# Three experts with few tokens: 64 slots and plain float32 products on two column tiles

## The chip, the core and the metric

The kernel runs on one core of a Trainium2 chip. The metric is the device time of one launch in microseconds, as the median of three runs. The engines are named as in the profile: PE (TensorE's products) and PEld (its weight loads), DVE (VectorE), ACT (ScalarE), POOL (GpSimd) and SP (SyncE, which issues the weight DMAs).

## What is computed

Two transformer blocks on 256 tokens of width 1024, in float32. The change lies in the mixture of experts of the first block's second layer:

```python
N_EXPERTS, TOP_K, D_EXPERT = 8, 2, 3584
def _moe(h, router, w1, w3, w2):
    logits = (hf @ router).astype(jnp.float32)
    top_v, top_i = lax.top_k(logits, TOP_K)
    top_w = jax.nn.softmax(top_v, axis=-1)
    gates = jnp.sum(jax.nn.one_hot(top_i, N_EXPERTS, dtype=jnp.float32) * top_w[..., None], axis=-2)
    for e in range(N_EXPERTS):
        y = y + gates[:, e:e + 1] * (jax.nn.silu(hf @ w1[e]) * (hf @ w3[e])) @ w2[e]
```

Each token goes to two of eight experts, so 512 token places are shared out unevenly. All of an expert's weights, 42 tiles of 1 MB, are read whatever its number of tokens.

## The kernel before

Weights come in tiles of 128 x 2048 float32 (1024 KB), each by one DMA that SP issues (`unit`, L238) into the next of `MOE_RING` = 6 buffers `raw`. SP works in order, so a load waits until the buffer's earlier contents are used up. Ordinary products use float32r: `split` makes of 1024 columns a rounded part `wh` (ACT, L245) and the rest `wl` (DVE, L246), four buffers of each, and `mm3` (L257 to L259) adds three products wh·xH, wl·xH, wh·xL. A `raw` buffer is free when its two halves are split.

`moe` ranks the experts: rank 0 is expert 0 whatever its count (`FIRST`), ranks 1 to 7 are the others by falling count. Rank 1 has 128 slots and 32 more (`CAP1` = 160), all others 128. `gather` (L1011) collects the tokens' rows in slots by products with a 0/1 matrix S and ACT evictions (L1024); `parts` (L1027) splits the rows in xeH and xeL (L1033, L1034); two ranks share a gather (`pair`, L1168).

`expert` (L1043) is a generator with one step per 512 hidden columns, seven in all and a rest. A step has four weight tiles for gate and up (48 products of 512 columns into two PSUM banks), SiLU (ACT, L1083), the multiplication (DVE, L1085), then two tiles of the down product for the step before (24 products), four transposes of the new hidden columns (L1109) and their split (L1112, L1113). The outputs are split and wait in `late`; `settle` multiplies them back to the tokens (L1148, L1149) while the next products run, and DVE adds them to y (L1158).

The 32 extra slots of rank 1 use another kind of product, plain float32 straight from `raw`: the stationary operand has 32 columns and the output takes 32 of PSUM's 128 partitions, so that four such products stand on four column tiles of the array (L1079 with 128 columns, L1103 with 256):

```python
for j in range(4):
    o = (kc % 4) * 512 + j * 128
    nc.tensor.matmul(px[32 * j:32 * j + 32, z * 128:(z + 1) * 128], xex[:, kc, :],
                     raw[:, o:o + 128], start=(kc == 0), stop=(kc == 7))
```

Order: rank 0 alone for five steps, then ranks 2 to 7 one after another, and after every fifth of their steps one step of rank 1 (L1201 to L1209). `ready` gathers an expert's rows before the last products of the one ahead of it (`run(g)`, L1203). After the stage the norms follow, and under `If(over > 0)` (L1245) a second pass of an expert whose tokens don't fit its slots, with a single weight buffer (`spare`).

Of the kernel before, what the change touches and what calls it, by code (L numbers as in the profile page):

```python
# [24 lines left out]
class Cols:  # L25
    """Columns of the small-parameter tile, in the order they are packed."""
# [30 lines left out]
def pack(inp):  # L57
# [42 lines left out]
    u = []  # L100
# [32 lines left out]
    for e in range(8):  # L133
# [15 lines left out]
        np.broadcast_to(np.where(r8 == 1, CAP1, 128).astype(np.float32), (128, 8))], axis=1)  # L149
# [65 lines left out]
CAP1 = 160  # L215
FF2_ORDER = [0, 2] + [u for i in range(2, 16) for u in (2 * i, 2 * i - 3)] + [29, 31]
# [4 lines left out]
class K:  # L221
# [19 lines left out]
    def split(self, src, n):  # L241
        """Exact split of fp32 data in two float32r parts."""
# [19 lines left out]
    def rsqrt(self, v, n):  # L262
        """1/sqrt(v) on [128, n] by Newton steps from the bit-pattern estimate."""
# [15 lines left out]
    def inv_rms(self, v, width):  # L279
        """1/sqrt(v / width) of a column v."""  # L280
# [18 lines left out]
    def diag(self, ys):  # L299
        """The diagonal matrices of two columns."""  # L300
# [18 lines left out]
def run(gen, n=None):  # L319
    """Advance a generator by n steps, or to its end."""  # L320
# [6 lines left out]
def ada_part(k, l, i):  # L327
    """Columns i*2048.. of silu(c) @ w_ada[l] + b_ada[l], for c (row 0) and c_ctx (row 1); a step per weight tile."""
# [31 lines left out]
def mod_cols(k, l, s):  # L360
    """A = g*(1+scale), B = shift as columns [128, 8, 2] for the s-th norm of layer l."""
# [8 lines left out]
class Sums:  # L370
    """Sums of squares of token rows, a column per half row."""
# [16 lines left out]
    def diag(self, t):  # L388
        """diag(1 / rms(x)) of token tile t."""
# [7 lines left out]
def mod_T(k, sums, A, B, H, L, by_tile=True):  # L397
    """Transposed A*xn + B of the four token tiles in two float32r parts; A, B: column 0 for x, 1 for ctx."""
# [288 lines left out]
def gain_T(k, ps, g, H, L):  # L687
    """Two float32r parts of ps * g (g per partition)."""
# [208 lines left out]
def moe(k):  # L897
# [12 lines left out]
    def order(v, lead, name):  # L910
        """How many entries come before each: greater ones, and equal ones of lower index."""
# [973 lines left out]
```

## Time and profile before

| | |
|---|---|
| median of three runs | 2372.45 us (2371.38 to 2373.67) |
| the profiled execution, its own span | 2374.5 us, 2.05 over the median |
| PE busy | 2290.1 us, 96% |
| PEld busy | 1810.7 us, 76% |
| DVE busy | 1736.9 us, 73% |
| ACT busy | 1282.0 us, 54% |
| DMA | 554.58 MB, mean 234 GB/s over the span |
| weight tiles of the experts | 336 of 1024.0 KB, 5.4 us from issue to landing |

The profile is of one execution. Busy shares are averages over stages with different limits, and PE's busy time overlaps itself, since a product's record is longer than the spacing between two of them. So the starts of neighbouring records tell TensorE's pace, and waits tell which engine or queue is ahead of which. A plain float32 product appears as two records.

### The profile page before, as it was taken

The page shows a single profiled execution, that of the slowest core. Times are in us where ns is not written, and L with a number is a line of the kernel's source. Part 1 is how long each engine was busy: PE and PEld are TensorE (multiplying, and loading weights), DVE is VectorE, ACT ScalarE, POOL GpSimd, SP SyncE. Part 2 cuts the span into 40 slices and gives each one's busy share as a digit, 9 for nine tenths or more (in the row PEclk, how much of TensorE's full clock was granted, in tenths as well). Part 3 has the DMA queues.
Part 4 walks back from the last instruction along what each step waited for, and adds up shares of the span by engine and source line. Part 5 has one row for each costly group of instructions (what it writes and reads, how often), then busy time and mean ns, then how long its engine had stood idle before and what let it go on. Part 6 is the DMA issues. An engine that isn't in the chain of part 4 may idle for free. (4 is left out here: it accounts for less than half of the span.)

```text
span 2374.5 us, 32425 instructions
## 1 busy us (share of the span) xinstructions
PE 2290.1 (96%) x12225; PEld 1810.7 (76%) x12225; DVE 1736.9 (73%) x2665; ACT 1282.0 (54%) x1709; POOL 49.5 (2%) x98
## 2 busy tenths in 40 slices
PE   6999999999999899999999999999999799999998
PEld 3767877788876777787877777778768587798997
DVE  3997359443665888897878788879788778776555
ACT  3234322222454677776767676767667644554444
POOL 1000000000000000000000000000000000000000
PEclk8999999999999999999999999999999899999999
DMA  9544445332540687897988888979779643344552
GB/s 371 225 162 162 180 151 195 129 124 91 201 169 32 235 340 299 300 374 280 366 316 323 309 343 327 359 283 353 306 267 362 254 158 111 125 146 156 190 188 78
DMA packets 82116, 554.58 MB, mean 234 GB/s; under 512 B 9904, under 2 KB 10160, under 8 KB 19232
## 3 DMA queue, kind: packets, MB, share of 16 engines
q1 hardware_dynamic: 75600, 531.87, 60.0%
q0 software_dynamic: 6208, 19.52, 2.4%
q8 instruction: 98, 1.61, 0.3%
q10 hardware_dynamic: 144, 1.05, 0.1%
q14 instruction: 66, 0.54, 0.1%
HBM read 546.08 MB, written 6.32 MB: 233 GB/s over the span
## 5 line engine op out<-in xcount | busy, mean ns | idle before, releaser
L246 DVE TENSOR_TENSOR wl<-raw,wh 128x1024 fp32r<-128x1024 f32 (+1 forms) x916 | 1097.5, 1218 | 371.1 <-ACT wh L245 360.7
L245 ACT CAST wh<-raw 128x1024 fp32r<-128x1024 f32 (+1 forms) x916 | 948.0, 1047 | 756.0 <-PE psA L259 217.7
L258 PE MATMUL psA<-wl,xeH 128*128 128x512 f32 x784 | 312.2, 398 | 2.1 <-DVE wl L246 2.1
L257 PE MATMUL psA<-wh,xeH 128*128 128x512 f32 x784 | 313.1, 400 | 0.4 <-ACT xf L1024 0.2
L259 PE MATMUL psA<-wh,xeL 128*128 128x512 f32 x784 | 310.5, 396 | 0.1
L258 PE MATMUL psO<-wl,hidH 128*128 128x512 f32 x480 | 190.7, 397 | 1.6 <-DVE wl L246 1.6
L259 PE MATMUL psO<-wh,hidL 128*128 128x512 f32 x480 | 189.8, 396 | 0.2 <-DVE hidL L1113 0.2
L257 PE MATMUL psO<-wh,hidH 128*128 128x512 f32 x480 | 185.1, 397 | 1.9 <-ACT hidH L1112 1.9
L258 PEld LDWEIGHTS psA<-wl,xeH 128*128 128x128 f32 x784 | 147.6, 188 | 40.9 <-DVE wl L246 7.4
L257 PEld LDWEIGHTS psA<-wh,xeH 128*128 128x128 f32 x784 | 147.7, 188 | 35.3 <-issue 0.6
L259 PEld LDWEIGHTS psA<-wh,xeL 128*128 128x128 f32 x784 | 147.6, 188 | 35.4 <-DVE xeL L1034 0.5
L257 PE MATMUL psG<-hH,wh 128*128 128x256 f32 x544 | 157.8, 290 | 0.9 <-DVE hL L690 0.9
L257 PE MATMUL psA<-xTH,wh 128*128 128x512 f32 x400 | 157.3, 393 | 0.0
L259 PE MATMUL psG<-hH,wl 128*128 128x256 f32 x544 | 155.8, 286 | 0.0
L258 PE MATMUL psA<-xTL,wh 128*128 128x512 f32 x400 | 155.7, 389 | 0.0
L259 PE MATMUL psA<-xTH,wl 128*128 128x512 f32 x400 | 155.7, 389 | 0.0
L258 PE MATMUL psG<-hL,wh 128*128 128x256 f32 x544 | 155.1, 285 | 0.0
L257 PEld LDWEIGHTS psG<-hH,wh 128*128 128x128 f32 x544 | 103.9, 191 | 13.2 <-issue 11.2
L257 PEld LDWEIGHTS psO<-wh,hidH 128*128 128x128 f32 x480 | 90.5, 189 | 24.9 <-ACT hidH L1112 2.3
L259 PEld LDWEIGHTS psG<-hH,wl 128*128 128x128 f32 x544 | 104.0, 191 | 6.3 <-issue 6.2
L258 PEld LDWEIGHTS psO<-wl,hidH 128*128 128x128 f32 x480 | 90.4, 188 | 22.7 <-DVE wl L246 2.0
L259 PEld LDWEIGHTS psO<-wh,hidL 128*128 128x128 f32 x480 | 90.5, 189 | 21.4 <-DVE hidL L1113 0.6
(564 smaller groups left out, 3664.8 us busy)
## 6 DMA issues: line engine op xcount, KB each, us to landing
raw<-in_moe_dram SPq DMA_DIRECT2D x336, 1024.0 KB, 5.4
raw<-in_w_ada_dram SPq DMA_DIRECT2D x48, 1024.0 KB, 6.1
raw<-in_w2ff_dram SPq DMA_DIRECT2D x32, 1024.0 KB, 4.8
raw<-in_w2mix_dram SPq DMA_DIRECT2D x24, 1024.0 KB, 4.9
raw<-in_eff_dram SPq DMA_DIRECT2D x22, 1024.0 KB, 4.9
raw<-in_eff_dram SPq DMA_DIRECT2D x22, 512.0 KB, 3.5
raw<-in_ein_dram SPq DMA_DIRECT2D x8, 1024.0 KB, 8.2
raw<-in_w2in_dram SPq DMA_DIRECT2D x8, 1024.0 KB, 4.9
```

The costliest lines, as they stand in the source:

```text
L245: self.nc.scalar.copy(h[:, :n], src)
L246: self.nc.vector.tensor_sub(l[:, :n], src, h[:, :n].bitcast(F32))
L257: mm(ps, s[0], m[0], start=first, stop=False)
L258: mm(ps, s[0], m[1], start=False, stop=False)
L259: mm(ps, s[1], m[0], start=False, stop=last)
```

## The change

Ranks 5, 6 and 7 (`SMALL`) get 64 slots instead of 128 and a generator of their own, `small_expert`. It splits no weights: its products take the `raw` tile as it lands, as plain float32, with 64 columns of stationary operand, and go in pairs to the two halves of PSUM's partitions (two column tiles of the array). A step has 32 products of 256 columns for gate and up into one bank, 8 of 512 columns for the down product, two transposes, and a copy of the hidden columns without a split. One gather of 192 slots serves all three. They are interleaved step by step with larger experts: rank 5 with rank 1, rank 6 with rank 2, rank 7 with rank 4 from its third step on; ranks 0 and 3 run alone. The large experts but rank 0 accumulate in the pool `pX`, the small ones in `pO`. The last expert is now a small one. Docstrings are dropped, so line numbers move by 9 to 11 (L245 is L254, L257 to L259 are L266 to L268, L1079 is L1090, L1103 is L1114, L1109 is L1120).

```diff
+SMALL = (5, 6, 7)
+LAST = 7
+def base_of(r):
+    return CAP1 if r == 1 else 64 if r in SMALL else 128
...
+    def gather(S, n=256, name="xf"):
+        xf = p.tile([128, 8, 256], F32, name=name)[:, :, :n]
...
-        tag = "hx" if extra is not None else "hid"
+        tag = "hid"
         if extra is not None:
             xex, SxT = extra
-            po = [k.pX.tile([128, 512], F32, name="psX") for _ in range(3)]
-        else:
-            po = [k.pO.tile([128, 512], F32, name="psO") for _ in range(2)]
+        pool, name = (k.pO, "psO") if r == 0 else (k.pX, "psX")
+        po = [pool.tile([128, 512], F32, name=name) for _ in range(2 if extra is None else 3)]
...
+    def small_expert(r, e, xf, i, Sd, mode="add"):
+        def src(u):
+            return a["moe"][ds(e, 1), u].rearrange("o p c -> (o p) c")
+        xs = slice(i * 64, (i + 1) * 64)
+        po = k.pO.tile([128, 512], F32, name="psO")
+        hid = None
+        for b in range(8):
+            if b < 7:
+                px = k.pA.tile([128, 512], F32, name="psA")
+                for z in range(2):
+                    for h in range(2):
+                        raw = k.unit(src(b * 4 + z * 2 + h))
+                        for kk in range(4):
+                            kc = 4 * h + kk
+                            for t in range(2):
+                                o = kk * 512 + t * 256
+                                nc.tensor.matmul(px[64 * t:64 * t + 64, z * 256:(z + 1) * 256], xf[:, kc, xs],
+                                                 raw[:, o:o + 256], start=(kc == 0), stop=(kc == 7))
+                m = k.tmp.tile([128, 512], F32, name="act", bufs=k.nact)
+                nc.scalar.activation(m[:, 0:256], px[:, 0:256], AF.Silu)
+                nc.vector.tensor_mul(m[:, 256:512], m[:, 0:256], px[:, 256:512])
+                settle()
+            if b > 0:
+                for u in (2 * b - 2, 2 * b - 1):
+                    raw = k.unit(src(28 + u))
+                    for q in range(2):
+                        c = u * 2 + q
+                        w = hid[:, (c % 2) * 128 + (c % 4) // 2 * 64:(c % 2) * 128 + (c % 4) // 2 * 64 + 64]
+                        for t in range(2):
+                            o = q * 1024 + t * 512
+                            nc.tensor.matmul(po[64 * t:64 * t + 64, :], w, raw[:, o:o + 512], start=(c == 0), stop=(c == 27))
+            if b < 7:
+                pt = k.pA.tile([128, 512], F32, name="psA")
+                for q in range(2):
+                    nc.tensor.transpose(pt[:, q * 128:(q + 1) * 128], m[:, 256 + q * 128:256 + (q + 1) * 128], k.ident)
+                hid = p.tile([128, 256], F32, name="hids", bufs=2)
+                nc.scalar.copy(hid, pt[:, :256])
+                yield True
+        settle()
+        o = po
+        if mode == "last":
+            o = k.tmp.tile([128, 512], F32, name="og", tag="act", bufs=k.nact)
+            for t in range(2):
+                ts_ = slice(64 * t, 64 * t + 64)
+                nc.vector.tensor_mul(o[ts_, :], po[ts_, :], k.gate5[ts_, t * 512:(t + 1) * 512])
+        oH = p.tile([128, 512], F32R, name="oH", tag="hidH", bufs=2)
+        oL = p.tile([128, 512], F32R, name="oL", tag="hidL", bufs=2)
+        nc.scalar.copy(oH, o)
+        nc.vector.tensor_sub(oL, o, oH.bitcast(F32))
+        def scatter():
+            for d in range(2):
+                for t in range(2):
+                    sl = slice(d * 512, (d + 1) * 512)
+                    ps = k.pA.tile([128, 512], F32, name="psA")
+                    ts_ = slice(d * 256 + t * 128, d * 256 + (t + 1) * 128)
+                    nc.tensor.matmul(ps, Sd[:, ts_], oH, start=True, stop=False)
+                    nc.tensor.matmul(ps, Sd[:, ts_], oL, start=False, stop=True)
+                    g = gater[:, t, r:r + 1]
+                    y = k.Xx if mode == "last" else k.y
+                    nc.vector.scalar_tensor_tensor(y[:, t, sl], ps, g, y[:, t, sl], op0=ALU.mult, op1=ALU.add)
...
-    todo = {}
-    def ready(r):
-        """The gathered slots of expert r, as operands."""
-        if r not in todo:
-            todo.update(zip((r, r + 1), pair(r)))
-        xf, z, ST = todo[r]
-        return parts(xf, z), ST
+    def smalls():
+        S = new_S()
+        for i, r in enumerate(SMALL):
+            slots(r, 0, S[:, :, i * 64:(i + 1) * 64], 64)
+        xf = gather(S, 64 * len(SMALL), "xs")
+        out = []
+        for i in range(len(SMALL)):
+            Sd = p.tile([128, 2, 2, 64], F32R, name="Sd", tag="Sx")
+            for t in range(2):
+                nc.vector.tensor_copy(Sd[:, t], S[:, t, i * 64:(i + 1) * 64].bitcast(F32).unsqueeze(1).to_broadcast([128, 2, 64]))
+            pt = k.pA.tile([128, 512], F32, name="psA")
+            for t in range(2):
+                nc.tensor.transpose(pt[:, t * 128:(t + 1) * 128],
+                                    Sd[:, t].rearrange("p j s -> p (j s)").bitcast(F32), k.ident)
+            Z = p.tile([128, 512], F32R, name="Sz", tag="Sz" if SMALL[i] == LAST else "hxH",
+                       bufs=1 if SMALL[i] == LAST else 2)
+            nc.gpsimd.memset(Z.bitcast(F32), 0.0)
+            for d in range(2):
+                d_ = slice(64 * d, 64 * d + 64)
+                nc.scalar.copy(Z[d_, d * 256:(d + 1) * 256], pt[d_, :256])
+            out.append((xf, i, Z))
+        return out
...
-    run(g, 5)
+    run(g, 4)
...
-    gx = expert(1, index(1), xe, STx, "add", (xex, SxT.bitcast(F32)))
-    n = 0
-    for r in range(2, 8):
-        xe, ST = ready(r)
-        run(g)
-        g = expert(r, index(r), xe, ST, "last" if r == 7 else "add")
+    todo = {1: expert(1, index(1), xe, STx, "add", (xex, SxT.bitcast(F32)))}
+    run(g, 1)
+    for r, made in zip(SMALL, smalls()):
+        todo[r] = small_expert(r, index(r), *made, "last" if r == LAST else "add")
+    run(g)
+    pairs = {}
+    def start(r):
+        if r in (2, 3, 4):
+            if r not in pairs:
+                pairs.update(zip((r, r + 1), pair(r)))
+            xf, z, ST = pairs[r]
+            todo[r] = expert(r, index(r), parts(xf, z), ST)
+    for one, other in ((1, 5), (2, 6), (3, None), (4, 7)):
+        start(one)
         for b in range(7):
-            run(g, 1)
-            n += 1
-            if n % 5 == 3:
-                run(gx, 1)
-            if r == 7 and b == 0:
-                for t in range(2):
-                    nc.vector.tensor_mul(k.y[:, t, :], k.y[:, t, :], k.gate5)
-                    nc.vector.tensor_add(k.Xx[:, t, :], k.Xx[:, t, :], k.y[:, t, :])
-        if r == 5:
+            run(todo[one], 1)
+            if other is not None and (other != LAST or b > 1):
+                run(todo[other], 1)
+        if one == 3:
             k.gate5 = gate_rows(k, 1, 5, 0)
             k.fg = k.tmp.tile([128, 1024], F32, name="fgr", tag="xn", bufs=k.nxn)
             nc.gpsimd.dma_start(k.fg, a["rowf"][0:1, :].to_broadcast([128, 1024]))
-        if r == 6:
-            run(gx)
-            over = nc.values_load(infoi[0:1, 16:17], engines=ALL_ENGINES, min_val=0, max_val=256)
+        run(todo[one])
+        if other not in (None, LAST):
+            run(todo[other])
+    over = nc.values_load(infoi[0:1, 16:17], engines=ALL_ENGINES, min_val=0, max_val=256)
+    run(todo[LAST], 1)
+    for t in range(2):
+        nc.vector.tensor_mul(k.y[:, t, :], k.y[:, t, :], k.gate5)
+        nc.vector.tensor_add(k.Xx[:, t, :], k.Xx[:, t, :], k.y[:, t, :])
+    run(todo[LAST], 1)
+    g = todo[LAST]
...
-        for r in range(4):
-            base = CAP1 if r == 1 else 128
+        for r in (0, 1, 2, 3) + SMALL:
+            base = base_of(r)
```

On TensorE, at the end of a step. `wh`, `wl` are split weights, `xe` the split rows, `hid` the split hidden columns of a large expert, `xs` the rows and `hids` the hidden columns of a small one. Before, in a step of a large expert, the transposes stand among the down products:

```order
L258 MATMUL psO<-wl,hidH 128x512
L259 MATMUL psO<-wh,hidL 128x512
L257 MATMUL psO<-wh,hidH 128x512 x2
L1109 MATMUL psA<-identt,act_12632 128x128 x4
L258 MATMUL psO<-wl,hidH 128x512
L259 MATMUL psO<-wh,hidL 128x512
```

Now, in the rounds of ranks 2 and 6, a whole small step stands between two large ones:

```order
L267 MATMUL psX<-wl,hidH 128x512
L268 MATMUL psX<-wh,hidL 128x512
L1192 MATMUL psA<-raw,xs 64x256 x32
L1210 MATMUL psA<-identt,act 128x128 x2
L1206 MATMUL psO<-raw,hids 64x512 x4
L1206 MATMUL psO<-raw_10407,hids 64x512 x4
L266 MATMUL psA<-wh,xeH 128x512
L267 MATMUL psA<-wl,xeH 128x512
```

The small step's transposes come right behind its 32 gate and up products, and its eight down products between them and the next large step.

In the rounds of ranks 1 and 5, the same place on TensorE now (L1090 are the extra slots' products):

```order
L1192 MATMUL psA<-raw,xs 64x256 x32
L1206 MATMUL psO<-raw,hids 64x512 x4
L1210 MATMUL psA<-identt,act 128x128 x2
L1206 MATMUL psO<-raw_8744,hids 64x512 x4
L266 MATMUL psA<-wh,xeH 128x512
L1090 MATMUL psA<-raw,xex 32x128 x13
L267 MATMUL psA<-wl,xeH 128x512
```

Here four of the eight down products stand ahead of the transposes.

On ACT, for the rounds of ranks 2 and 6. Before, in a step of a large expert, the casts of the next weights stand on both sides of every other instruction:

```order
L245 CAST wh<-raw 128x1024 x4
L1083 ACTIVATE act<-psA 128x512
L245 CAST wh<-raw 128x1024 x2
L245 CAST wh<-raw_11497 128x1024 x2
L245 CAST wh<-raw 128x1024 x2
L1112 CAST hidH<-psA 128x512
```

Now:

```order
L254 CAST wh<-raw_10534 128x1024 x2
L1123 CAST hidH<-psA 128x512
L1195 ACTIVATE act<-psA 128x256
L1212 COPY hids<-psA 128x256
L254 CAST wh<-raw 128x1024 x6
L1094 ACTIVATE act<-psA 128x512
```

The casts for the next large step stand behind the small step's SiLU (L1195) and the copy of its hidden columns (L1212).

## Rows read from the trace of the kernel before

**Rows 1.** Windows of the expert stage: length, busy time by engine (instructions), clock, DMA share, GB/s

```profile
1020.00:1060.00 40.00, 40.00 (x178) 32.22 (x177) 36.53 (x33) 31.17 (x34) 0.00 (x0) 1.00 0.98 373
1100.00:1200.00 100.00, 100.00 (x515) 77.68 (x514) 82.66 (x77) 71.40 (x77) 0.00 (x0) 1.00 0.90 346
1130.00:1170.00 40.00, 40.00 (x179) 32.37 (x178) 35.24 (x32) 30.00 (x32) 0.00 (x0) 1.00 0.97 381
1300.00:1400.00 100.00, 100.00 (x569) 77.40 (x568) 82.34 (x78) 71.11 (x77) 0.00 (x0) 1.00 0.86 329
1820.00:1840.00 20.00, 20.00 (x92) 16.20 (x91) 16.87 (x16) 14.43 (x16) 0.00 (x0) 1.00 0.98 360
790.00:1886.00 1096.00, 1080.31 (x5631) 838.14 (x5631) 924.19 (x914) 790.21 (x879) 0.99 (x2) 0.99 0.85 322
```

**Rows 2.** Waits of the DMA queue on SP: us in total, times, longest

```profile
SPq L238 <- DVE wl L246: 1427.2, 388, 59.6
```

**Rows 3.** Timeline of PE, one step: start, us, instruction, count

```profile
1288.60 0.39 PE L259 MATMUL psO<-wh,hidL 128*128 128x512 f32 x1
1288.83 0.60 PE L1109 MATMUL psA<-identt,act 128*128 128x128 f32 x4
1289.18 0.48 PE L257 MATMUL psA<-wh,xeH 128*128 128x512 f32 x1
...
1306.07 0.60 PE L1109 MATMUL psA<-identt,act 128*128 128x128 f32 x4
1306.42 0.48 PE L257 MATMUL psA<-wh,xeH 128*128 128x512 f32 x1
1306.74 0.39 PE L258 MATMUL psA<-wl,xeH 128*128 128x512 f32 x1
1306.97 0.39 PE L259 MATMUL psA<-wh,xeL 128*128 128x512 f32 x1
```

**Rows 4.** Timeline of PE, the stage's first gather and last scatter

```profile
790.13 0.98 PE L1022 MATMUL psA<-S,xnH 128*128 128x256 f32 x3 [1.45 <-ACT wh L245]
...
1886.48 0.40 PE L1149 MATMUL psA<-oL,ST 128*128 128x512 f32 x1
```

**Rows 5.** Timeline: plain float32 products on the whole array, and on four column tiles

```profile
700.68 1.88 PE L824 MATMUL psA<-xTL,qT 128*128 128x512 f32 x4
702.49 0.70 PE L827 MATMUL psA<-kpT,qr 64*128 64x512 f32 x2
...
1106.34 0.40 PE L259 MATMUL psA<-wh,xxL 128*128 128x512 f32 x1
1106.66 0.81 PEld L1079 LDWEIGHTS psA<-raw,xex 128*32 128x32 f32 x32 [0.37 <-issue]
1106.66 1.08 PE L1079 MATMUL psA<-raw,xex 128*32 128x128 f32 x32
1107.68 0.50 PE L257 MATMUL psX<-wh,hxH 128*128 128x512 f32 x1
1108.02 0.39 PE L258 MATMUL psX<-wl,hxH 128*128 128x512 f32 x1
...
1108.95 0.39 PE L259 MATMUL psX<-wh,hxL 128*128 128x512 f32 x1
1109.27 0.64 PE L1103 MATMUL psX<-raw,hxx 128*32 128x256 f32 x8
1109.84 0.50 PE L257 MATMUL psX<-wh,hxH 128*128 128x512 f32 x1
1110.17 0.40 PE L258 MATMUL psX<-wl,hxH 128*128 128x512 f32 x1
```

**Rows 6.** Groups by shape, ACT and DVE, 800 to 1886: count | busy, mean ns

```profile
L245 ACT CAST wh<-raw 128x1024 fp32r<-128x1024 f32 x668 | 691.8, 1051 | 213.5 <-PE psA L259 131.1 <-PE psO L259 49.5 <-PE psX L259 28.9
L1024 ACT ACTIVATE xf<-psA,mx,modA 128x256 f32<-128x256 f32 x32 | 16.4, 566 | 3.0 <-PE psA L1022 1.9 <-DVE xxL L1034 0.9
L1033 ACT CAST xeH<-xf 128x512 fp32r<-128x512 f32 x12 | 7.5, 623 | 0.1
L1008 ACT CAST ST<-psA 128x256 fp32r<-128x256 f32 x7 | 2.6, 368 | 7.8 <-PE psA L1149 7.8
...
L246 DVE TENSOR_TENSOR wl<-raw,wh 128x1024 fp32r<-128x1024 f32 x668 | 799.3, 1223 | 120.5 <-ACT wh L245 112.5
L1085 DVE TENSOR_TENSOR act<-act,psA 128x512 f32<-128x512 f32 x56 | 38.3, 684 | 16.6 <-PE psA L259 16.6
L1034 DVE TENSOR_TENSOR xeL<-xf,xeH 128x512 fp32r<-128x512 f32 x12 | 8.2, 686 | 6.1 <-ACT xeH L1033 6.1
```

**Rows 7.** DMA issues of the page; windows at the start; L334's longest wait

```profile
raw<-in_moe_dram SPq DMA_DIRECT2D x336, 1024.0 KB, 5.4
...
5.00:30.00 25.00, 14.35 (x72) 3.42 (x72) 3.61 (x23) 5.91 (x17) 1.99 (x4) 0.86 1.02 404
30.00:55.00 25.00, 19.66 (x109) 15.63 (x106) 18.14 (x53) 16.74 (x37) 3.60 (x7) 0.79 0.98 388
...
  DMA raw<-in_w_ada_dram: 41.6, 17
```

**Rows 8.** Groups of weight loads by shape, 800 to 1886

```profile
L1079 PEld LDWEIGHTS psA<-raw,xex 128*32 128x32 f32 x896 | 23.1, 109 | 11.5 <-issue 11.2 <-DVE wl L246 0.4
L257 PEld LDWEIGHTS psA<-wh,xeH 128*128 128x128 f32 x780 | 146.9, 188 | 34.8 <-issue 0.6
```

More of the change, by code (lines that the diff above doesn't have):

```diff
@@ L148, in pack @@
         np.broadcast_to((r8 == FIRST) * np.float32(1024), (128, 8)),
-        np.broadcast_to(np.where(r8 == 1, CAP1, 128).astype(np.float32), (128, 8))], axis=1)
+        np.broadcast_to(np.array([base_of(r) for r in range(8)], np.float32), (128, 8))], axis=1)
     out["rowf"] = np.stack([f["final_g"], f["norm_final_2"]])
@@ L964, in permuted @@
         out = p.tile(sh3, F32, name=name)
-        w = p.tile([128, 2, 8, 8], F32, name="permw2")
+        w = p.tile([128, 2, 8, 8], F32, name="permw2", tag="tke")
         nc.vector.tensor_tensor(w, v.unsqueeze(2).to_broadcast([128, 2, 8, 8]),
@@ L1009, in slots_T @@
         return ST
-    def gather(S):
-        xf = p.tile([128, 8, 256], F32, name="xf")
+    def gather(S, n=256, name="xf"):
+        xf = p.tile([128, 8, 256], F32, name=name)[:, :, :n]
         for d2 in range(4):
@@ L1017, in gather, with parts @@
                 d = d2 * 2 + z
-                zs = slice(z * 256, (z + 1) * 256)
-                n = 0
+                zs = slice(z * n, (z + 1) * n)
+                i = 0
                 for x in (xnH, xnL):
                     for t in range(2):
-                        nc.tensor.matmul(ps[:, zs], x[:, t, d * 128:(d + 1) * 128], S[:, t, :], start=(n == 0), stop=(n == 3))
-                        n += 1
+                        nc.tensor.matmul(ps[:, zs], x[:, t, d * 128:(d + 1) * 128], S[:, t, :n], start=(i == 0), stop=(i == 3))
+                        i += 1
                 nc.scalar.activation(xf[:, d, :], ps[:, zs], AF.Identity, scale=A[:, d, 0:1], bias=B[:, d, 0:1])
         return xf
-    def parts(xf, z, name="xe", bufs=2):
-        H = p.tile([128, 8, 128], F32R, name=name + "H", bufs=bufs)
-        L = p.tile([128, 8, 128], F32R, name=name + "L", bufs=bufs)
+    def parts(xf, z, rest=False):
+        if rest:
+            HL = p.tile([128, 8, 256], F32R, name="xr", tag="xs")
+            H, L = HL[:, :, 0:128], HL[:, :, 128:256]
+        else:
+            H, L = [p.tile([128, 8, 128], F32R, name="xe" + part, bufs=2) for part in "HL"]
         for d in range(0, 8, 4):
@@ L1160, in expert @@
         late.append(scatter)
+    def small_expert(r, e, xf, i, Sd, mode="add"):
[58 more added lines that the diff above has]
+                    nc.vector.scalar_tensor_tensor(y[:, t, sl], ps, g, y[:, t, sl], op0=ALU.mult, op1=ALU.add)
+        late.append(scatter)
@@ L1190, in moe @@
     xf = gather(S)
-    xe = parts(xf, 0, "xx", 1)
+    xe = parts(xf, 0)
     xex = p.tile([128, 8, 32], F32, name="xex")
@@ L1229, in moe @@
             else:
-                hl.append(p.tile([128, 8, 128], F32R, name="w0" + part, tag="xx" + part, bufs=1).rearrange("p d s -> p (d s)"))
+                hl.append(p.tile([128, 8, 128], F32R, name="w0" + part, tag="xe" + part, bufs=2).rearrange("p d s -> p (d s)"))
         o = (0, 1024, 1536)[z]
@@ L1252, in moe @@
                     slots(r, base, S[:, :, z * 128:(z + 1) * 128])
-                xe = parts(gather(S), 0)
+                xe = parts(gather(S), 0, True)
                 run(expert(r, index(r), xe, slots_T(S[:, :, 0:128], f"STf{r}"), "last"))
```

2 lines of the change are left out of this document (removed).

## The prediction

> **What bounds the kernel now.** I read the views in this order: windows over the expert stage, the DMA queue's own waits, the timeline of one step, and the groups by shape. In the windows [rows 1] the reader is to see that from 790 to 1886 us TensorE is busy 1080.31 of 1096 us at clock 0.99, while the DMA share lies between 0.85 and 0.98. That leaves two candidates. The queue's waits settle it [rows 2]: SyncE spends 1427.2 us of the run waiting until the split on VectorE has emptied a weight buffer, so the loads wait for the buffers and the buffers for the products. The timeline [rows 3] gives the pace: neighbouring 512-column products start 0.23 us apart, and one step (six 1 MB weight tiles, 72 products, four transposes) takes 1306.07 - 1288.83 = 17.24 us. VectorE needs 12 x 1.223 us for a step's splits and ScalarE 12 x 1.051 [rows 6], 14.7 and 12.6, and both wait. So the stage, 790.13 to 1886.48 [rows 4], is bound by TensorE; but a step asks for 6 x 1.0486 MB in 17.24 us, 365 GB/s, and the DMAs are the next limit close behind.
>
> **The sum.** It is made against the profiled execution, whose span is 2374.5 us; the median of the three runs, 2372.45, is 2.05 lower.
>
> *Removed.* Three experts of seven steps at 17.24: 21 x 17.24 = -362.
>
> *Added: 21 small steps.* Their products are plain float32 on column tiles, which the old kernel has for the 32 extra slots of rank 1, there on four tiles of 32 columns. Two places give the price [rows 5]. Sixteen such products of 128 columns (32 records: each product stands there twice) push the next ordinary product from 1106.34 to 1108.02; without them it would be two spacings, 0.46, so they cost 1.22. Four of 256 columns (8 records) cost 1110.17 - 1108.95 - 0.46 = 0.76. With f for going to the tiles and back and c for a pass of 128 columns on all tiles at once, 8c + f = 1.22 and 4c + f = 0.76: c = 0.115, f = 0.30. That the tiles run side by side is seen from a plain float32 product on the whole array: four records of 512 columns take 702.49 - 700.68 = 1.81, so 0.45 each and 0.11 for 128 columns, which is c. One pass on four tiles costs no more than one record on the whole array. I take the same for two tiles of 64 columns. A small step has 32 products of 256 columns: 64 passes, two at a time, 32 x 2c = 7.36. It has 8 of 512: 8 x 4c = 3.68. It goes to the tiles twice (the transposes stand between): 2f = 0.60. Two transposes are half of 0.35 [rows 3]: 0.18. In the new order these follow the last gate product at once, so they wait for the multiplication on VectorE: a 256-column half of 0.684 [rows 6] and a handing-on of about as much, 0.7 in all (0 if a down product had stood there, 1.3 if SiLU must wait too). Sum 12.5 us, 21 x 12.5 = +262. Ends: 11.8 and 13.1, which is 248 and 275.
>
> The weight loads of such a product are taken at nothing: in the group of 32 they are busy 0.81 us under 1.08 us of products [rows 5]. The Trainium skill, page "TensorE: Matmul & The Clock Gate", section on the mechanism of packing, says that a load overlaps running products only where the row group differs, which column tiles do not offer. Here the trace disagrees; by that rule, with the page's 64 / 1.2 ns for a load, 40 loads a step would add 2.1 us a step, an estimate, and the sum would end 45 us higher. As a mechanism priced from rows it is a rival below.
>
> *Splits.* 21 x 12 splits leave ScalarE and VectorE. Neither sets the pace, so this counts 0.
>
> *Handing over from small to large.* ScalarE works in order; the next large step's casts stand behind the small step's SiLU and copy, so no weights lie split when the small step ends. After the transposes come the copy (0.37), a cast (1.05) and a subtraction (1.22) [rows 6], with signals about 3 us. Opposite ranks 2 and 4 eight down products, 3.68 us, cover this: 0. Opposite rank 1 only four or none do, with some extra products behind: I take 0.7 x 7 = 5. Ends: 0, and 2.3 x 19 = 44 if nothing covers it.
>
> *Borders.* The gather of ranks 2 and 3 used to run under the last products of the expert ahead; now it stands between two pairs, and ScalarE's evictions and splits of rows (0.566, 0.623, VectorE 0.686) [rows 6] lie on the path: +4, between 0 and 8. The small experts' gather takes the place of one of the pairs', and scatters stay as many: 0. The tail after the last scatter does not change: 0.
>
> So far -362 + 262 + 5 + 4 = -91, if weights are always there.
>
> *Weights.* A round of large and small takes 17.24 + 12.5 = 29.7 us and reads 12 tiles, 12.58 MB: 423 GB/s. What the DMAs can do is seen at the start, where products wait for them: 404, then 388 GB/s (products wait 41.6 us for the modulation's weights) [rows 7]. In the expert stage 373 and 381 are seen with TensorE as the limit [rows 1], so these are a floor. A round of loads thus takes 31.1 to 33.0 us; I take the middle, 32.1, 2.4 above the products. Ranks 2 with 6 and 4 with 7 make 14 such rounds: 34. Each pair starts behind a stretch bound by TensorE with the ring full, some four tiles or 10.7 us ahead: -21. That leaves +12 (0 at 404 GB/s, +25 at 381). The round of rank 1 takes 17.24 + 4 x 1.22 + 4 x 0.76 + 12.5 = 37.7 and is not reached by this.
>
> Total -79: 2374.5 - 79 = 2295.5, and against the median **2293 us**. With all ends at their best it is 2258 (-362 + 248 + 0 + 0 + 0 = -114), with all at their worst 2362 (-362 + 275 + 44 + 8 + 25 = -10), and they hardly come together.
>
> **Rivals.**
> *The DMAs take over wholly.* A small tile's buffer is freed by products, not by splits, so the ring may starve in bursts. If the stage's ends count, 360 to 373 GB/s as a ceiling: 34.9 us a round, 5.2 x 14 = 73 in place of 12, no lead: 2354. For it: the share of 0.98 at 373 [rows 1]. Against: that window is TensorE's pace, and 404 has been seen.
> *Handing over is never covered.* 2.3 us at each of 21 small steps, +48 in place of 5, 2336. For it: ScalarE's order. Against: the eight down products.
> *Weight loads lie open (slower).* If each of the 40 passes a step waited for its load, between the 0.109 of 32 columns and the 0.188 of 128 [rows 8], say 0.13: 5.2 us a step, 109 in all; the rounds are then long enough for the DMAs, so 2293 + 109 - 12 = 2390. It decides from (79 + 12) / (21 x 40) = 0.108 us a pass on. Against: [rows 5], where passes of 128 columns follow each other at c = 0.115 with their loads hidden. This is what the skill's rule above would mean here.
> *Two tiles do not run side by side (slower).* Then 11.04 us of products become 22.1: 232 more, 2293 + 232 - 12 = 2513. Against: four tiles do [rows 5].
> *The change does not do what it says.* If one of the last three experts had more than 64 tokens, the branch for overflow would run one more expert alone, its 42 tiles one after another through a single buffer, each landing in 5.4 us [rows 7] and split before the next is asked for: over 42 x 7.7 = 323 us, some 2616. The reference's router gives 71, 42, 56, 76, 50, 24, 134 and 59 tokens on its input, so 24, 42 and 50 are the smallest three: no.
>
> **Chances.** Forecast as worked out (2255 to 2345) 0.77, DMAs wholly 0.10, handing over 0.06, loads open 0.04, tiles in turn 0.02, overflow 0.01. The range 2255 to 2345 holds the first and the third, 0.83. A measurement of this kernel can tell 0.2%, 4.7 us, from no change. The first three are faster, 0.93, of which 0.01 goes to no change for their upper tail; the last three are slower, 0.07.
>
> **What the profile after would show.** Right: groups of 32 products 64x256 some 7.4 us long, small steps near 12.5 us and large ones at 17.24; 252 splits fewer on each of ScalarE and VectorE; the expert stage some 80 us shorter; windows of the pairs at 385 to 405 GB/s with waits of TensorE on weight DMAs or none. Wrong: small steps of 18 us or more (loads or tiles), TensorE waiting for casts after every small step (handing over), or pairs at 360 GB/s with long waits on DMAs.

## The result, and the profile after

The changed kernel takes **2272.6 us** (median of four runs, 2268.23 to 2274.87) against 2373.06 for the kernel before in the same rounds: a ratio of 0.9571, 95% interval 0.9557 to 0.9585. Faster was forecast, at 2293 within 2255 to 2345; the gain is 20 us larger than worked out. The profiled execution has a span of 2269.8 us and took 2272.78.

The page of the changed kernel: busy time by engine, then two groups and the DMA issues of the expert weights.

```profile
span 2269.8 us, 31775 instructions
...
PE 2167.8 (96%) x12353; PEld 1639.3 (72%) x12353; DVE 1413.6 (62%) x2391; ACT 1007.1 (44%) x1452; POOL 51.0 (2%) x101
...
L255 DVE TENSOR_TENSOR wl<-raw,wh 128x1024 fp32r<-128x1024 f32 x664 | 791.5, 1215 | 379.3 <-ACT wh L254 372.8
L254 ACT CAST wh<-raw 128x1024 fp32r<-128x1024 f32 x664 | 679.3, 1045 | 651.6 <-PE psA L267 176.0
...
raw<-in_moe_dram SPq DMA_DIRECT2D x336, 1024.0 KB, 7.4
```

As many tiles are loaded as before, but 664 casts and subtractions are left of 916, 252 fewer on each engine. A tile now lands 7.4 us after its issue, not 5.4 [rows 7]: loads stand behind each other. The stage shows where. Its windows: ranks 1 with 5, ranks 2 with 6, rank 3 alone, ranks 4 with 7 (length; busy time of PE, PEld, DVE, ACT and POOL, each with its instructions; granted clock, DMA share, GB/s).

```profile
1020.00:1175.00 155.00, 155.00 (x1314) 96.55 (x1316) 65.10 (x68) 55.94 (x68) 1.05 (x2) 1.00 0.88 337
1250.00:1410.00 160.00, 154.18 (x870) 103.21 (x869) 79.50 (x77) 70.57 (x84) 0.00 (x0) 1.00 1.01 418
1460.00:1545.00 85.00, 84.68 (x373) 67.20 (x372) 71.93 (x67) 62.45 (x70) 0.00 (x0) 1.00 0.95 358
1610.00:1740.00 130.00, 124.50 (x703) 84.49 (x702) 65.55 (x64) 58.30 (x70) 0.00 (x0) 0.99 0.98 398
```

Before, TensorE was busy throughout with DMAs at 0.85 to 0.98 [rows 1]. In the two pairs the share is now 0.98 to 1.01, up to 418 GB/s, and TensorE has gaps. The timeline of one round of ranks 2 and 6 (PE: start, duration, group, idle before it with its releaser) is the counterpart of the step in [rows 3].

```profile
1335.66 0.60 PE L1120 MATMUL psA<-identt,act 128*128 128x128 f32 x4
...
1339.93 7.13 PE L1192 MATMUL psA<-raw,xs 128*64 128x256 f32 x64
1347.99 0.44 PE L1210 MATMUL psA<-identt,act 128*128 128x128 f32 x2 [0.94 <-DVE act L1196]
1348.36 3.65 PE L1206 MATMUL psO<-raw,hids 128*64 128x512 f32 x16
1351.94 0.50 PE L266 MATMUL psA<-wh,xeH 128*128 128x512 f32 x1
...
1365.48 0.60 PE L1120 MATMUL psA<-identt,act 128*128 128x128 f32 x4
```

The small step runs from 1339.93 to 1351.94, 12.0 us. The round takes 1365.48 - 1335.66 = 29.82 us and reads twelve tiles: 2.485 us each, or 422 GB/s. A round of ranks 4 and 7 is a little shorter:

```profile
1664.01 0.60 PE L1120 MATMUL psA<-identt,act 128*128 128x128 f32 x4
1693.57 0.60 PE L1120 MATMUL psA<-identt,act 128*128 128x128 f32 x4
```

That is 29.56 us, which e2 below shows to be TensorE's own pace. The stage goes from 790.26 to 1784.46 us: 994.2 in place of 1096.4 [rows 4], 102 less. That is where nearly all of the gain lies (the spans differ by 104.7). Two queries give the groups of TensorE in the stage (busy, mean ns, idle before them, by releaser); the first row is of its weight loads.

```profile
L1192 PEld LDWEIGHTS psA<-raw,xs 128*64 128x64 f32 x1344 | 94.5, 137 | 53.0 <-issue 5.3 <-DMA raw<-in_moe_dram 0.9 <-PE psA L1120 0.7
...
L266 PE MATMUL psA<-wh,xeH 128*128 128x512 f32 x560 | 228.3, 408 | 2.7 <-ACT wh L254 1.2 <-ACT xeH L1045 1.1 <-ACT xf L1033 0.2
L267 PE MATMUL psA<-wl,xeH 128*128 128x512 f32 x560 | 226.3, 404 | 4.4 <-DVE wl L255 4.4
L1192 PE MATMUL psA<-raw,xs 128*64 128x256 f32 x1344 | 150.3, 381 | 0.8 <-DMA raw<-in_moe_dram 0.4 <-DVE y L1165 0.3
...
L1206 PE MATMUL psO<-raw,hids 128*64 128x512 f32 x336 | 79.5, 608 | 3.1 <-DMA raw<-in_moe_dram 3.1
...
L1210 PE MATMUL psA<-identt,act 128*128 128x128 f32 x42 | 9.2, 300 | 12.3 <-DVE act L1196 12.2
```

The largest wait is the one before the small step's transposes (L1210), 12.2 us in all. Before the gate and up products of the large steps (L266 and L267 into `psA`) TensorE idles 7.1 us, 5.6 of them for split weights.

### The profile page after: what moved, and what is told of

Read it like the earlier page. It is cut to its first block, busy times and chain, and to the rows that moved or that the text cites. A ratio compares the mean times of both kernels' runs of the same rounds, so it can differ in the third digit from the quotient of the medians.

```text
span 2269.8 us, 31775 instructions
## 1 busy us (share of the span) xinstructions
PE 2167.8 (96%) x12353; PEld 1639.3 (72%) x12353; DVE 1413.6 (62%) x2391; ACT 1007.1 (44%) x1452; POOL 51.0 (2%) x101
## 5 line engine op out<-in xcount | busy, mean ns | idle before, releaser
L255 DVE TENSOR_TENSOR wl<-raw,wh 128x1024 fp32r<-128x1024 f32 x664 | 791.5, 1215 | 379.3 <-ACT wh L254 372.8
L254 ACT CAST wh<-raw 128x1024 fp32r<-128x1024 f32 x664 | 679.3, 1045 | 651.6 <-PE psA L267 176.0
L266 PE MATMUL psA<-wh,xeH 128*128 128x512 f32 x560 | 228.3, 408 | 2.7 <-ACT wh L254 1.2
L267 PE MATMUL psA<-wl,xeH 128*128 128x512 f32 x560 | 226.3, 404 | 4.4 <-DVE wl L255 4.4
L268 PE MATMUL psA<-wh,xeL 128*128 128x512 f32 x560 | 223.1, 398 | 0.1
L266 PE MATMUL psG<-hH,wh 128*128 128x256 f32 x544 | 157.8, 290 | 1.0 <-DVE hL L699 1.0
L266 PE MATMUL psA<-xTH,wh 128*128 128x512 f32 x400 | 157.3, 393 | 0.0
L268 PE MATMUL psG<-hH,wl 128*128 128x256 f32 x544 | 155.8, 286 | 0.0
L267 PE MATMUL psA<-xTL,wh 128*128 128x512 f32 x400 | 155.7, 389 | 0.0
L268 PE MATMUL psA<-xTH,wl 128*128 128x512 f32 x400 | 155.7, 389 | 0.0
L267 PE MATMUL psG<-hL,wh 128*128 128x256 f32 x544 | 155.1, 285 | 0.0
L1192 PE MATMUL psA<-raw,xs 128*64 128x256 f32 x1344 | 150.3, 381 | 0.8 <-DMA raw<-in_moe_dram 0.4
L266 PEld LDWEIGHTS psA<-wh,xeH 128*128 128x128 f32 x560 | 106.3, 190 | 41.1 <-ACT wh L254 11.3
L1192 PEld LDWEIGHTS psA<-raw,xs 128*64 128x64 f32 x1344 | 94.5, 137 | 53.0 <-issue 5.3
L267 PEld LDWEIGHTS psA<-wl,xeH 128*128 128x128 f32 x560 | 106.5, 190 | 35.9 <-DVE wl L255 12.2
L268 PEld LDWEIGHTS psA<-wh,xeL 128*128 128x128 f32 x560 | 106.3, 190 | 25.0 <-DVE xeL L1046 0.9
L266 PEld LDWEIGHTS psG<-hH,wh 128*128 128x128 f32 x544 | 103.9, 191 | 13.3 <-issue 11.2
L268 PEld LDWEIGHTS psG<-hH,wl 128*128 128x128 f32 x544 | 103.9, 191 | 6.3 <-issue 6.2
L267 PEld LDWEIGHTS psG<-hL,wh 128*128 128x128 f32 x544 | 104.0, 191 | 3.3 <-issue 2.7
L266 PEld LDWEIGHTS psA<-xTH,wh 128*128 128x128 f32 x400 | 75.1, 188 | 25.4 <-ACT wh L254 8.4
L267 PE MATMUL psX<-wl,hidH 128*128 128x512 f32 x224 | 89.9, 401 | 0.0
```

The costliest lines, as they stand in the source:

```text
L254: self.nc.scalar.copy(h[:, :n], src)
L255: self.nc.vector.tensor_sub(l[:, :n], src, h[:, :n].bitcast(F32))
L266: mm(ps, s[0], m[0], start=first, stop=False)
L267: mm(ps, s[0], m[1], start=False, stop=False)
L268: mm(ps, s[1], m[0], start=False, stop=last)
L1192: nc.tensor.matmul(px[64 * t:64 * t + 64, z * 256:(z + 1) * 256], xf[:, kc, xs], raw[:, o:o + 256], start=(kc == 0), stop=(kc == 7))
```

## The experiments

Two limits seemed to stand within 0.3 us of each other in a pair's round: TensorE at 29.6, the DMAs at 29.82. The first three kernels, run on one chip, take one off, then the other, then both.

**Later transposes** (e1). In `small_expert`:

```diff
+            if b > 0:
+                pt = k.pA.tile([128, 512], F32, name="psA")
+                for q in range(2):
+                    nc.tensor.transpose(pt[:, q * 128:(q + 1) * 128], m[:, 256 + q * 128:256 + (q + 1) * 128], k.ident)
+                hid = p.tile([128, 256], F32, name="hids", bufs=2)
+                nc.scalar.copy(hid, pt[:, :256])
             if b < 7:
...
-                nc.scalar.copy(hid, pt[:, :256])
                 yield True
```

> The small expert's transposes and the copy of its hidden values are issued at the start of its next step instead of at the end of the same step; nothing else moves. So TensorE no longer waits for SiLU and multiplication (1.2 us a small step in the changed kernel's timeline) before it goes on. Theory A (in the 14 rounds of ranks 2 with 6 and 4 with 7 the weight DMAs set the pace, 12 tiles x 2.485 us = 29.82): those rounds stay at 29.6 to 29.8 us, TensorE waits for casts or raw tiles in place of the multiply, and only the 7 rounds opposite rank 1 (37.4 us, DMA not full) can gain, up to 1.2 each: 0 to -9 us against the change, 2264 to 2273. Rival B (TensorE sets the pace there too and 29.8 is its own sum): every round gains 1.2, rounds of 28.5 us, -25 us, 2248.

2269.53 us (2268.08 to 2273.45), which the noise doesn't tell from the change. It is what theory A said, and so is a round of ranks 2 and 6, as long as it was: 1335.58 - 1305.69 = 29.89.

```profile
1305.69 0.60 PE L1120 MATMUL psA<-identt,act 128*128 128x128 f32 x4
1335.58 0.60 PE L1120 MATMUL psA<-identt,act 128*128 128x128 f32 x4
```

The groups of TensorE in the stage of this run show where the saved wait went:

```profile
L266 PE MATMUL psA<-wh,xeH 128*128 128x512 f32 x560 | 228.0, 407 | 8.6 <-ACT wh L254 7.1 <-ACT xeH L1045 1.1 <-ACT xf L1033 0.2
L267 PE MATMUL psA<-wl,xeH 128*128 128x512 f32 x560 | 226.3, 404 | 9.4 <-DVE wl L255 9.4
...
L1186 PE MATMUL psA<-identt,act 128*128 128x128 f32 x42 | 8.3, 279 | 2.9 <-DVE act L1202 2.8
```

Before the transposes 9.4 us are saved (12.2 to 2.8), and the next large step's first products wait 10.9 longer (18.0 against 7.1). The waits of this run from 800 to 1800 us name what stands behind them:

```profile
ACT wh L254 <- DMA raw<-in_moe_dram: 45.4, 40, 7.5
```

In the change the casts wait 22.8 us for tiles in the same stretch. So the wait was not removed but, as it seems, handed on to tiles that had not landed; e7 below tests that.

**Small steps spread** (e2). The order only:

```diff
-    for one, other in ((1, 5), (2, 6), (3, None), (4, 7)):
+    small = iter([5] * 7 + [6] * 7 + [7] * 5)
+    for one in (1, 2, 3, 4):
...
+            if one == 1 or (n - 7) * 12 // 21 > (n - 8) * 12 // 21:
+                other = next(small)
```

> Only the order changes: 12 of the 14 small steps of ranks 6 and 7 that stood opposite ranks 2 and 4 are dealt out evenly over the 21 large steps of ranks 2, 3 and 4 (rank 3 had none); rank 5 stays opposite rank 1, the last two small steps stay at the end, rank 6's seventh comes earlier. A large step then carries 0.57 small ones: 9.4 tiles, 23.4 us of DMA at 2.485 us a tile, against 24.4 us of products (17.24 + 0.57 x 12.5). Theory A (DMA and TensorE are almost equally long in the pair rounds, so neither alone is worth much): TensorE becomes the bound by 1 us a step, the DMA share in the stage falls to about 0.93, the time stays within -6 to +4 us, 2267 to 2277. Rival B (the DMAs hold the rounds back by much, hidden in stretched products): -15 us or more, 2257 or less. Rival C (handing over from small to large costs more where no down products cover it): +10 or more.

2264.81 us (2261.08 to 2266.75), 8 below the change, 2 more than theory A allowed. Measured again on the chip of this run (e10 below), the change took 2269.83, so 5 of the 8 are the safer figure. A round with a small step:

```profile
1640.13 0.60 PE L1120 MATMUL psA<-identt,act 128*128 128x128 f32 x4
1669.69 0.60 PE L1120 MATMUL psA<-identt,act 128*128 128x128 f32 x4
```

It takes 29.56 us though a round without a small step follows and the loads have time: that is TensorE's own sum, the wait before the transposes included. The rows place some 3 us of the gain (L267 waits 1.9 us for split weights in place of 4.4); where the rest comes from stays open.

**Both** (e3).

> Both edits: transposes and copy later, and the small steps of ranks 6 and 7 dealt out over ranks 2, 3 and 4. Theory A (two limits almost equal: either edit alone meets the other limit, both together pass): the wait of 1.2 us goes at each of 21 small steps and the DMAs, 23.4 us a step against 23.7 of products, no longer stop it: -18 to -25 us against the change, 2248 to 2255, clearly more than the sum of the two alone. Rival B (TensorE alone binds): the same as the later transposes alone, -25 each. Rival C (the DMA queue's order or handing over is what binds): no more than -8.

2262.55 us (2260.28 to 2267.43): -10 against the change as first measured, half of what was expected, and not told from e2 by the noise. A round with a small step:

```profile
1638.56 0.60 PE L1120 MATMUL psA<-identt,act 128*128 128x128 f32 x4
1666.82 0.60 PE L1120 MATMUL psA<-identt,act 128*128 128x128 f32 x4
```

Such rounds fall to 28.26 us, which neither edit does alone; the time hardly follows. The expectation took the wait to stand in 21 small steps. In rank 5's rounds the instruction order put the down products ahead of the transposes, so those seven had no wait: only the 12.2 us were ever there, and the group of the transposes shows 2.8 left. Against e2 that is 9.8 us less (12.6 there), but some 6 of them come back: by the same view TensorE idles 8.3 us before L266 and L267 (4.4 in e2), 1.9 before the small gate and up products (0.3) and 3.6 before the small down products (3.1).

**No interleaving** (e4).

```diff
     for one in (1, 2, 3, 4):
         start(one)
-        for b in range(7):
-            run(todo[one], 1)
...
+        run(todo[one], 7)
...
+    for other in (5, 6):
+        run(todo[other])
+    run(todo[LAST], 5)
```

> The small experts are no longer interleaved: ranks 1, 2, 3, 4 run alone, then ranks 5, 6 and the first five steps of 7, then the end as it was. The products are the same. Theory A (a small step alone is 12.5 us of products but asks for six tiles, 14.9 us at 2.485 us a tile; a large step asks for the same six in 17.24): about 19 small steps are bound by DMAs and lengthen by 2.4 us, +46 us, and the wait for the multiply (1.2 us) hides under that; +35 to +55 us against the change, 2308 to 2328, and small steps of 14.9 us. Rival B (the interleaving buys nothing but order): 0 +- 5 us, 2273. Rival C (the ring of buffers starves when six are freed in bursts): small steps of 17 us and more, +85 us or more.

2314.11 us (2312.23 to 2316.17), +41.5: theory A. Two small steps in a row start their transposes 14.91 us apart:

```profile
1643.43 0.44 PE L1210 MATMUL psA<-identt,act 128*128 128x128 f32 x2 [0.94 <-DVE act L1196]
1658.34 0.44 PE L1210 MATMUL psA<-identt,act 128*128 128x128 f32 x2 [0.94 <-DVE act L1196]
```

The window over small steps alone, then TensorE's waits in the run:

```profile
1600.00:1700.00 100.00, 81.40 (x562) 39.11 (x558) 6.04 (x11) 5.12 (x13) 0.00 (x0) 1.00 1.01 421
```

```profile
PE psA L1192 <- DMA raw<-in_moe_dram: 34.6, 60, 1.7
...
PE psA L1210 <- DVE act L1196: 21.2, 21, 2.3
PE psO L1206 <- DMA raw<-in_moe_dram: 5.3, 5, 3.1
```

421 GB/s with TensorE idle a fifth of the time and waiting for tiles is the DMAs' ceiling here, seen without a rival limit. The wait before the transposes stands in all 21 steps, as it doesn't in the change.

**Half the loads** (e7), the later transposes with:

```diff
                     for h in range(2):
-                        raw = k.unit(src(b * 4 + z * 2 + h))
+                        if h == 0 or r == 5:
+                            raw = k.unit(src(b * 4 + z * 2 + h))
```

> As the run with the later transposes (2269.5 us), and ranks 6 and 7 load only two of the four gate and up tiles of a step and use each for both halves of the contraction; products and their number stay, the small experts' results do not. So a round of ranks 2 with 6 and 4 with 7 asks for 10 tiles, 24.9 us at 2.485, in place of 12, 29.82. Theory A (the DMAs refused the later transposes their gain there): rounds fall from 29.8 to 17.24 + 11.06 = 28.3 us, some 12 of them, -15 to -20 us against that run, 2250 to 2255. Rival B (the casts behind the small step's SiLU on ScalarE, the handing over, refuse it): rounds stay within 0.4 us of 29.8, 2262 or more.

2245.71 us (2242.97 to 2248.1), 24 below e1, 4 more than theory A allowed. Rounds of ranks 4 and 7:

```profile
1648.38 0.60 PE L1120 MATMUL psA<-identt,act 128*128 128x128 f32 x4
1676.64 0.60 PE L1120 MATMUL psA<-identt,act 128*128 128x128 f32 x4
```

28.26 us; in e1 three such rounds take 29.59, 30.35 and 32.41. With the loads out of the way the later transposes gain what they promised, so the loads, not ScalarE's order, had refused it. Up to the last small step the two profiled executions differ by 1769.52 - 1750.57 = 19 us, as theory A has it; what the rest behind it comes from stays open.

**Column tiles not in turns** (e5): the loop over the two tiles goes outside the loop over `kk` (and over `q` for down products).

```diff
-                        for kk in range(4):
-                            kc = 4 * h + kk
-                            for t in range(2):
+                        for t in range(2):
+                            for kk in range(4):
+                                kc = 4 * h + kk
```

> Only the order of the small experts' products changes: for each weight tile all four products of the left column tile come first, then all four of the right one (down products: two and two), where before the two column tiles took turns product by product. The number of products, loads and the results are the same. Theory A (the two column tiles run side by side because neighbouring products lie on different tiles, 0.107 us a product record at 64x256): with four products, eight records, in a row on one tile, they no longer overlap, a record of 256 columns costs its own 0.21 us and only the seams overlap; a step's 11.06 us of products become 20 to 22: +120 to +220 us against the change (as far as the DMAs' 14.9 us a step had not covered it), 2390 to 2490. Rival B (TensorE's queue looks past a product that waits for its tile, so the order does not matter): 2273 +- 5.

2292.42 us (2290.77 to 2293.4), +20: neither, but far nearer to B. The 64 records of a step, from the timeline, last 8.38 us where the change needs 7.13:

```profile
1353.31 8.38 PE L1192 MATMUL psA<-raw,xs 128*64 128x256 f32 x64
```

Windows of 0.92 us over these records alone (busy time and records, clock, DMA share, GB/s):

```profile
1353.30:1354.22 0.92, 0.91 (x4) 1.00 1.00 419
1354.22:1355.14 0.92, 0.92 (x9) 1.00 1.01 419
1355.14:1356.06 0.92, 0.92 (x10) 1.00 1.03 427
```

(Records that run on from the stretch before count in both.) First only four records begin in 0.92 us, one tile's own pace. Then the other tile's products start, while the first still has four of its eight records to go. So later products on a free tile pass a few waiting ones; the alternation saves some 1.2 us a step, not 10.

**The products undone** (e6): ranks 5 to 7 as ordinary 128-slot experts, in the change's order.

```diff
-    return CAP1 if r == 1 else 64 if r in SMALL else 128
+    return CAP1 if r == 1 else 128
...
+        if r in SMALL:
+            S = new_S()
+            slots(r, 0, S[:, :, 0:128])
+            xs = gather(S, 128, "xs")
...
```

> Undoes the products and keeps the order: ranks 5, 6 and 7 run as 128-slot experts with three float32r products on split weights, as in the kernel before, but interleaved with ranks 1, 2 and 4 step by step as in the change, each with a gather of its own. Theory A (the gain lies in the small experts' products, 12.5 us a step in place of 17.24; the order by itself is worth nothing and the DMAs at 12 tiles in 34.5 us are not full): 2373, between 2365 and 2385. Rival B (a good part of the gain is the order: gathers, scatters and casts lie better): 2350 or less. Rival C (the step-by-step order costs by itself, which the change pays too): 2390 or more.

2392.47 us (2391.15 to 2394.47), ratio to before 1.0078 (1.0063 to 1.0094): +19, rival C by its number. Its gathers explain much of it, which the expectation had left out: with a gather of its own for each of ranks 5 to 7 there are seven in place of five.

```profile
L1031 PE MATMUL psA<-S,xnH 128*128 128x256 f32 (+1 forms) x112 | 26.3, 318 | 7.2 <-ACT xs L1033 3.7 <-ACT xf L1033 1.9 <-ACT wh L254 1.4
L1031 PE MATMUL psA<-S,xnL 128*128 128x256 f32 (+1 forms) x112 | 24.3, 306 | 0.0
```

Five gathers are 80 such records of each kind, 19.1 and 16.5 us busy, in the change, so the two more account for 15.0 of the 19. The order by itself therefore gains nothing; whether it costs a few microseconds is open. The gain is in the products and in what goes with them, the splits that are no longer made.

**Two versions from the findings.** The first (e8) makes rank 4 a fourth small expert:

```diff
-SMALL = (5, 6, 7)
+SMALL = (4, 5, 6, 7)
```

> A version from the findings: rank 4 (56 tokens) becomes a fourth small expert. Each of rank 1's seven steps carries two small steps (ranks 4 and 5), 12 of the small steps of ranks 6 and 7 are dealt out over the 14 large steps of ranks 2 and 3, the last two stay at the end; transposes later. Sum: seven steps of 17.24 go and seven of 11.06 come, -43 against the run with both edits (2262.6). DMA: a step of ranks 2 and 3 now asks for 6 + 0.857 x 6 = 11.1 tiles, 27.7 us at 2.485, against 17.24 + 0.857 x 11.06 = 26.7 of products: up to +14. One border with its gather goes: -5 to -10. Theory A (both limits as measured): 2215 to 2235. Rival B (two small steps behind each other starve the ring or the next large step's casts): 2240 or more.

2641.65 us (2634.34 to 2647.34): the overflow branch ran. The token counts that the prediction quotes are the router's on the inputs before the reference scales some of them. On the real inputs they are 76, 16, 133, 68, 53, 11, 77 and 78: rank 4 has 68, over its 64 slots. The three smallest, 53, 16 and 11, still fit. The run does give the price of one overflow, a rival of the prediction: ACT's groups from 1790 to 2190 us show casts waiting 181 us for 42 tiles through the one spare buffer.

```profile
L254 ACT CAST wh<-spare 128x1024 fp32r<-128x1024 f32 x84 | 83.7, 1043 | 181.2 <-DMA spare<-in_moe_dram 181.1
```

The second (e9) uses the real counts: 32 slots and four column tiles for ranks 6 and 7.

```diff
+SLOTS = {5: 64, 6: 32, 7: 32}
...
+            if one == 1:
+                run(todo[5], 1)
+                run(todo[6], 1)
+            elif (n - 7) * 5 // 21 > (n - 8) * 5 // 21:
+                run(todo[next(small)], 1)
```

> A version from the findings. Of the reference's real input the three smallest experts have 53, 16 and 11 tokens, so ranks 6 and 7 get 32 slots and products on four column tiles of 32, as rank 1's extra slots have; that halves their products. Order: each of rank 1's seven steps carries one step of rank 5 and one of rank 6, five steps of rank 7 are dealt out over the 21 steps of ranks 2 to 4, two stay at the end; transposes later. Sum by the limits as measured: a step of rank 1 carries 25.2 + 11.1 + 0.9 + 6.2 = 43.4 us of products and 18 tiles, 44.7 us at 2.485; a step of ranks 2 to 4 17.3 + 0.24 x 6.2 = 18.8 of products and 7.4 tiles, 18.5. So 7 x 44.7 + 21 x 18.8 = 708 in place of the 758 that the run with both edits needs there (7 x 37.3 + 21 x 17.3 + 12 x 11.1): -50, 2213. Theory A (both limits as measured, the ring of six tiles carries over): 2205 to 2225. Rival B (two small steps behind each other drain the ring, or the next large step's casts come late each time, 2 to 3 us in each of seven rounds and more at the borders): 2230 to 2245. Rival C (products on 32 columns do not shrink with the slots): 2255 or more.

2287.47 us (2284.65 to 2300.04): slower than the change, and a time that only C had named. C is not its cause: 32 records of 32 columns take 1.08 us, as rank 1's extra products do [rows 5].

```profile
1065.89 1.08 PE L1201 MATMUL psA<-raw,xs 128*32 128x128 f32 x32 [0.33 <-DMA raw<-in_moe_dram]
```

Parts of one round, whose transposes start at 1051.56 and 1105.71, 54.15 us apart, in windows of 5 us:

```profile
1045.00:1050.00 5.00, 5.00 (x35) 2.93 (x32) 0.52 (x1) 0.00 (x0) 0.00 (x0) 1.00 0.74 274
1050.00:1055.00 5.00, 4.83 (x42) 3.01 (x42) 0.98 (x2) 0.86 (x2) 0.00 (x0) 1.00 0.76 261
...
1065.00:1070.00 5.00, 2.72 (x87) 1.92 (x76) 0.17 (x1) 0.28 (x1) 0.00 (x0) 1.00 1.03 431
1070.00:1075.00 5.00, 3.49 (x32) 1.28 (x32) 0.12 (x1) 0.00 (x0) 0.00 (x0) 0.50 1.00 416
1075.00:1080.00 5.00, 3.31 (x32) 2.00 (x29) 2.83 (x3) 3.54 (x4) 0.00 (x0) 0.50 1.01 423
...
1090.00:1095.00 5.00, 5.00 (x50) 3.80 (x49) 4.58 (x4) 3.10 (x4) 0.00 (x0) 1.00 0.74 239
```

My sum gave a round 18 tiles x 2.485 = 44.7 us, as if the loads averaged over it. Under rank 1's large step the DMAs run at 0.74. The DMA queue's waits from 1083 to 1120 us say why: no buffer is free, since rank 1's products hold them.

```profile
SPq L248 <- PE psA L1091: 16.0, 4, 5.2
SPq L248 <- PE psX L1115: 7.2, 2, 3.7
```

Under the small steps they run at 1.0 and TensorE waits for tiles. After those waits the clock is granted at 0.50, the 1.2 GHz level, for 10 us and more. Both are in the 54 us. e8 holds them apart in part: there a round of rank 1 has the same 18 tiles beside two steps of 64 slots, the clock stays at 1.00 (1049 to 1101 us), and the round takes 1100.90 - 1049.29 = 51.61 us, more than its loads (44.7) and, by the same sum, its products (25.2 + 2 x 11.1 + 0.9 = 48.3). So uneven loads seem to cost some 3 us there at full clock. That e9 has 4.9 us less of products in a round and still takes 2.5 us longer goes with its lower clock, but no run changes the clock alone.

**The change again** (e10), beside the 32-slot version.

> The change itself again, on the same chip and in the same rounds as the 32-slot version, to compare them directly: 2273 +- 3.

2269.83 us (2266.71 to 2275.41), so e9 is 18 us slower on one chip. Of the versions that load all the weights e3 has the lowest time, 7 us below e10 (same chip) and 10 below the change as first measured; its ratio to before is 0.9544 (0.953 to 0.9558), beside e2's 0.9547 (0.9534 to 0.956).

## Why the prediction was right, and where its sum was off

- **Removed, -362.** Right: TensorE set the pace before, and a large step alone still takes 17.3 us.
- **Small steps, 12.5 us.** Near in sum, 12.0, in part by luck: two errors offset each other. Gate and up products last 7.1 us at most (7.36 forecast), and products, transposes and the trips to the column tiles together take 10.8 in place of 11.8. The wait for the multiplication is 1.2 to 1.3 where it stands (29.56 in e2 against 28.26 in e3), the upper end and not 0.7: SiLU reads the gate half alone, but starts at 1347.10, behind the last of the 64 records. Opposite rank 1 down products stand there and the wait is 0; such a round takes 1100.60 - 1063.19 = 37.4 (37.7 forecast).
- **Weight loads at nothing.** Right: 137 ns each, beside products that follow each other at 7.13 / 64 = 0.11 us. By the rule of the Trainium skill ("TensorE: Matmul & The Clock Gate", the mechanism of packing) loads on column tiles would not overlap; the trace disagrees again, now at 64 columns. (A product's two records have a load each, 1344 = 21 x 64 for gate and up alone, so the prediction's 40 loads a step are 80, and its estimate by that rule would be twice as large.)
- **Two tiles side by side.** Right, and e5 adds that it hardly needs the order that was thought its condition.
- **Handing over, +5.** Right: TensorE idles 7.1 us before gate and up products where it idled 2.5 in the kernel before, so +4.6; 3.5 of it is for split weights.
- **Weights, +12.** This step failed, in its size. It took 392 GB/s, between 404 at the start [rows 7] and 381 of a window where TensorE set the pace. The ceiling is 421 to 422 (e4, and the rounds themselves), so a round of loads is 29.82 us, not 32.1, and only 0.1 over the products as forecast: some +1 in place of +12. The trace of the kernel before held it. Its window from 30 to 55 us, whose mean is the 388, cut into 40 slices:

```profile
GB/s 420 419 419 419 420 419 419 419 420 419 419 419 420 419 419 419 420 419 419 446 393 380 419 419 367 131 354 419 419 406 419 419 446 249 98 288 367 387 380 354
```

While the weight loads follow without a break the rate is 419 to 420; behind that, gaps between them and, at the end, the transfers of another queue pull the mean down. Nor is the DMA share a rate: 0.98 stood beside 373 GB/s before [rows 1] and stands beside 398 now. The sum also counted 14 rounds where the order gives 12, since rank 7 joins rank 4 from the third step on. That it would be the loads which are next was right in the rounds of ranks 2 and 6, as e1 and e7 show; those of ranks 4 and 7 stayed at TensorE's pace.
- **Borders, +4.** The stage shrank by 102, not 79. An estimate from the steady rounds places most of the 23: a small step adds 37.41 - 25.17 = 12.24 us opposite rank 1 (whose step alone takes 25.17 in e4), 29.82 - 17.24 = 12.58 opposite rank 2 and 29.56 - 17.24 = 12.32 opposite rank 4; with 12 for the two at the end that is 7 x 12.24 + 7 x 12.58 + 5 x 12.32 + 2 x 12 = 259, where the sum had 262 + 5 + 12 = 279. So 20 of the 23 lie in the rounds, 11 of them in the term for weights. The other 3 are left to the borders, some +1 in place of +4, and were not measured by themselves.
- **Overflow.** The counts quoted for it were the wrong ones (see e8). The conclusion held; the price of 323 us was low: in e8's timeline the transposes of the overflowing expert follow each other every 51 us (1858.35, 1909.52), 357 for seven steps, where 6 x 7.7 = 46 was forecast.

## What to carry to other kernels

When a change shortens the work of an engine, divide the bytes of the new pace by the best rate that the same transfers reach with nothing else in the way; a rate seen under another limit, or a mean over mixed transfers, is a floor, and here the ceiling lay 8% above the rate taken. Where two limits are nearly equal, lifting one can show nothing in the time (e1): look at the rounds, and take the other away too (e3, e7). In e9 the loads did not balance over a round of 18 tiles with a ring of six; whether a longer ring would cure it was not tested. There the engine that waited for tiles seems to have paid a second time, in its clock.

## What was not expected of the hardware

Products on a column tile that is free begin ahead of earlier ones that wait for another tile: with eight records in a row on one tile e5 lost 1.25 us of gate and up products a step (8.38 against 7.13), where one record after the other, four in 0.92 us, would have come to 64 x 0.23 = 14.7 us. And the granted clock stayed at 1.00 in e4, with TensorE busy 81% and waits of up to 1.7 us, while in e9 it fell to 0.50 after a stretch of 5 us with 2.72 busy.
